# Down projection by Strassen's scheme, with split factors made once and kept in DRAM

## The chip, the cores and the metric

The program runs on one core of one Trainium2 chip. The metric is device time in microseconds (us) for one launch; lower is better. Engines are named as in the profile: PE (TensorE), PEld (its weight loads), DVE (VectorE), ACT (ScalarE), POOL (GpSimd), SP (SyncE, which issues most DMAs).

## What is computed

One decoder layer over 2048 prompt tokens and 32 sample tokens (2080 columns in all), in float32. What matters here is the channel mixer:

```
hn = rmsnorm(h)                         # 1024 features
u  = hn @ w_gate                        # 1024 -> 2816
c  = conv_b + 3-tap causal conv of u over tokens
h  = h + (silu(c) * (hn @ w_up)) @ w_down   # 2816 -> 1024
```

Ahead of it stand the input projections (a @ w_in, seven groups of 512 features), a gated linear recurrence, dilated attention and the output projection; behind it a gated embedding and a final norm.

## The kernel before, in words

Features lie on partitions, tokens on the free axis. A float32 operand is split into hi (rounded to the type that PE reads in one pass) and lo (the rest), and a product is three matmuls, hi\*hi, hi\*lo, lo\*hi: `mm3`, lines 136 to 138. So nearly every matmul of the program has one of these lines, and the tiles tell them apart.

- **Phase 0** (`in_phase(0, ...)`, first 1024 tokens): seven weight groups one after the other; a group's 8 weight tiles of 128x512 are loaded by SP (line 220), rounded on POOL (line 142) and subtracted on DVE (line 224). There are 4 buffers for raw tiles and 9 for rounded ones, so the last tiles of a group are loaded while PE changes over to it. Results leave by stores on SP (lines 265, 330, 337 to 342). Phase 1 does the same for the other 1056 tokens, with the recurrence (`hgrn_unit`) beside it; then come attention and sample work.
- **Trunk** (`trunk`): tokens in three blocks (`TRUNK`: 704, 704, 672). First the output projection for all blocks, then the channel mixer for all blocks (`ffn_block`), then the embedding (`embed_block`). A dense weight tile 128x512 comes by SP into a `raw` buffer, ACT copies its hi (line 909), DVE subtracts its lo (line 910).
- **Channel mixer of a block**: 22 feature tiles of 128, taken as 11 pairs. For a pair, gate and up are each one Strassen product of 2x2 quarters (`quarters`, `strassen`): seven products of 4 x 3 matmuls over half of the block's tokens, the sums of weight quarters on POOL (lines 1103 to 1111), the sums of results on DVE and ACT. The token factors of the block's input are made by `ffn_prep` at the change of block, ahead of the first pair. After conv, silu and gating (`gms`), the pair's activations are split (lines 1256 to 1259).
- **Down projection** (`downs`): for each pair, 8 output tiles x 2 token halves x 2 feature tiles x 3 matmuls = 96 matmuls, each result in a PSUM bank of its own, which DVE adds to `h` (line 1171). The weights of the pair are loaded and split anew in every block (4 tiles of 128x512). The 16 steps go into a queue `todo`; `down(n)` emits the next n of them between the products of the following pair's gate and up, as the tuples `gate` and `up` in `ffn_block` say. Steps left at a block's end are emitted in the next block's first pair.

The order on each engine is set by a list scheduler from program order, priorities and its own costs, so neighbouring work mixes more finely than the code.

Of the kernel before, what the change touches and what calls it, by code (L numbers as in the profile page):

```python
# [11 lines left out]
F32 = mybir.dt.float32  # L12
# [25 lines left out]
TRUNK = ((0, 704, 704), (704, 704, 704), (1408, 672, 640))  # L38
LAST = 256
LEVELS = (1, 4, 16)  # L40
USE = (1, 5, 6, 7, 4, 2, 3)
AHEAD = 1000
# [3 lines left out]
def hymba_step_kernel(ctx: ExitStack, tc: tile.TileContext, I: dict, O: dict):  # L46
# [37 lines left out]
    mix_d = dram.tile([128, NK, NTOK], F32, name="mix_d")  # L84
    h_d, hn_d, h2_d = [dram.tile([128, NK, NTOK], F32, name=n) for n in ("h_d", "hn_d", "h2_d")]
# [62 lines left out]
    def copy_after(ins, n=1):  # L148

        with tc.issue_after(ins.ins):  # L150
            for _ in range(min(n, len(copies))):
                src, dst, b, r = copies.pop(0)
                lo, hi = 292 * r, 292 * (r + 1)
                A.dma_start(O[dst][b, lo:hi], I[src][b, lo + 4:hi + 4])

# [21 lines left out]
    def in_phase(bi, tiles, shared, wp, ev, sm, pmm, pms, plv, po):  # L177
# [63 lines left out]
        def feature_group(g, kind, dst, w):  # L241
            todo = [(m, c0, cn) for c0, cn in chunks for m in range(4)]
            while todo:
# [10 lines left out]
                for (m, c0, cn), ps in zip(cur, pss):  # L254
# [10 lines left out]
                    SP.dma_start(dst[:, m, t0 + c0:t0 + c0 + cn], o)  # L265
# [14 lines left out]
        def token_group(g, kind, w):  # L280
            late = None

            for j in (0, 1, 8, 2, 3, 4, 5, 6, 7) if bi else range(8):
# [33 lines left out]
                if kind in "qk":  # L317
                    rotate(o, 16 if smp else tok // 128, n)

                    def late(o=o, n=n, smp=smp, tok=tok):  # L320
# [6 lines left out]
                        else:  # L327
                            oT = ev.tile([128, 4, 128], F32, name="oT", bufs=2)
                            V.tensor_copy(oT, ptv)
                            SP.dma_start((qT_d if kind == "q" else kT_d)[:, :, tok:tok + 128], oT)  # L330
# [4 lines left out]
                else:  # L335
                    if kind == "k":
                        SP.dma_start(O["pk"][tok:tok + 128], o)
                    if kind == "v":
                        SP.dma_start(O["pv"][tok:tok + 128], o)
                        SP.dma_start(v_d[tok:tok + 128], o)  # L340
# [557 lines left out]
    def trunk(cst, rp, ev, sm, tw, hp, sh, wp, pmm):  # L898
# [8 lines left out]
        def split(raw):  # L907
            w = wp.tile([128, 2, 512], F32R, name="w")
            A.copy(w[:, 0], raw)  # L909
            V.tensor_sub(w[:, 1], raw, f32(w[:, 0]))  # L910
            return w

        def weight(src):
            return [split(load(src[:, 512 * i:512 * i + 512])) for i in range(2)]
# [4 lines left out]

        def acc_tile():  # L920
            return pmm.tile([128, 512], F32, name="mm")

        def wide(T, dt=F32):
            return tw.tile([128, 704], dt, name="w")[:, :T]

        def held(T, dt=F32):
            return hp.tile([128, 704], dt, name="h")[:, :T]
# [170 lines left out]
        def quarters(src, f):  # L1098

            a11, a12, a21, a22 = [load(src[f + i][:, 512 * j:512 * j + 512]) for i in range(2) for j in range(2)]  # L1100
            w = {1: split(a11)}
            s1, s2 = raw_tile(), raw_tile()
            G.tensor_add(s1, a21, a22)  # L1103
            w[5] = split(s1)
            G.tensor_sub(s2, s1, a11)
            w[6] = split(s2)
            G.tensor_sub(a21, a11, a21)
            w[7] = split(a21)
            w[4] = split(a22)
            w[2] = split(a12)  # L1110
            G.tensor_sub(s2, a12, s2)  # L1111
            w[3] = split(s2)
            return w

        def strassen(w, X, H, put, after, before=lambda n: None):
# [8 lines left out]
            def copied():  # L1124
                t = sh.tile([128, 352], F32, name="s")[:, :H]
# [3 lines left out]
            pa, pb, pc = acc_tile(), acc_tile(), acc_tile()  # L1129
# [23 lines left out]
        def downs(b, f, parts, h):  # L1153
# [3 lines left out]
            w = [[], []]  # L1157

            def more():
                for i in range(2):  # L1160
                    j = len(w[i])
                    w[i].append(split(load(I["w_down"][f + i][:, 512 * j:512 * j + 512])))

            def one(m, c0):
                if (m, c0) == (2, 0):
                    more()
                cs = slice(c0, c0 + H)
                ps = acc_tile()
                for i, (hi, lo) in enumerate(parts):
                    mm3(ps[:, :H], *piece(w[i], m), hi[:, cs], lo[:, cs], i == 0, i == 1)  # L1170
                V.tensor_add(h[m][:, cs], h[m][:, cs], ps[:, :H])  # L1171
                if f == NF - 2 and c0:
                    SP.dma_start(h2_d[:, m, t0:t0 + T], h[m])

            more()
# [469 lines left out]
```

## Time and profile before

| | us |
|---|---|
| runs shown: median (lowest to highest) | 3101.7 (3099.03 to 3104.79) |
| the profiled execution's own time | 3096.28 |
| its span, first to last instruction | 3094.5 |
| PE busy | 2992.3 |
| DVE busy | 2233.4 |
| ACT busy | 1295.2 |
| POOL busy | 806.6 |

A matmul's record is longer than its turn on PE, since matmuls are pipelined: what one costs is read from how many fit into a stretch. Idle time of an engine matters only where PE waits for it.

### The profile page before, as it was taken

Reading aid. Unit: us, or ns where it says so; the run is one execution under the profiler, and the core shown is the slowest. Engines: PE = TensorE matmul, PEld = TensorE weight load, DVE = VectorE, ACT = ScalarE, POOL = GpSimd, SP = SyncE. Lnnn points to the kernel's source line nnn. Section 1 sums busy time; section 2 is a strip of 40 time slices with the busy share of each in tenths; the row PEclk is TensorE's granted clock in tenths of the full one; section 3 lists DMA queues with packets and bytes.
Section 4 is the critical chain, followed back from the end, with each engine's and each line's share of the span. In section 5 each row is a group of like instructions: output and inputs, shape, how many; then the busy total and the mean of one; then the engine's idle time right before and its main releaser. Section 6 shows DMA issues by size and latency. Waiting matters only on the chain.

```text
span 3094.5 us, 52057 instructions
## 1 busy us (share of the span) xinstructions
PE 2992.3 (97%) x19035; PEld 2785.2 (90%) x19035; DVE 2233.4 (72%) x4662; ACT 1295.2 (42%) x2813; POOL 806.6 (26%) x659
## 2 busy tenths in 40 slices
PE   9999999999889989999999999999999999999997
PEld 8988899987675667998999998999998999999997
DVE  7424667867587686568777779777789877777776
ACT  4111422222276564335444444444445444445443
POOL 1111122222343342002222232222222222222331
PEclk9999999999999999999999999999999999999998
DMA  5234333342539976673443445333434444436443
GB/s 185 93 121 135 105 104 104 106 141 81 158 79 284 285 225 218 237 265 139 137 133 113 133 156 168 124 126 131 144 119 162 153 139 139 144 116 219 132 166 130
DMA packets 265216, 467.97 MB, mean 151 GB/s; under 512 B 39360, under 2 KB 107072, under 8 KB 263168
## 3 DMA queue, kind: packets, MB, share of 16 engines
q1 hardware_dynamic: 261376, 397.66, 40.7%
q10 hardware_dynamic: 3584, 66.98, 6.1%
q8 instruction: 150, 2.46, 0.3%
q14 instruction: 106, 0.87, 0.1%
HBM read 381.05 MB, written 150.48 MB: 172 GB/s over the span
## 4 chain that ended last, share of the span: by engine, by line
PE 80%; DVE 12%; DMA 3%; issue 2%; ACT 1%; POOL 1%; SPq 0%; DVEq 0%; ACTq 0%; POOLq 0%
PE mm L136 18%; PE mm L137 18%; PE mm L138 18%; PE mm L301 3%; PE mm L302 3%; PE mm L303 3%; PE acc L744 1%; PE lv L441 1%; PE PT L732 1%; DVE w L910 1%; DVE P L724 1%; PE lv L301 1%; PE lv L303 1%; PE lv L302 1%; PE S L719 1%
## 5 line engine op out<-in xcount | busy, mean ns | idle before, releaser
L137 PE MATMUL mm<-w 128*128 128x352 f32 (+3 forms) x3768 | 1212.4, 322 | 4.3 <-DVE w L982 4.3
L138 PE MATMUL mm<-w 128*128 128x352 f32 (+3 forms) x3640 | 1164.0, 322 | 0.0
L136 PE MATMUL mm<-w 128*128 128x352 f32 (+3 forms) x3640 | 1138.7, 323 | 18.2 <-ACT w L981 8.7
L137 PEld LDWEIGHTS mm<-w 128*128 128x128 f32 x3768 | 712.9, 189 | 8.0 <-DVE w L982 7.8
L136 PEld LDWEIGHTS mm<-w 128*128 128x128 f32 x3640 | 681.8, 189 | 24.6 <-ACT w L981 10.6
L910 DVE TENSOR_TENSOR w<-raw,w 128x512 fp32r<-128x512 f32 x718 | 563.1, 799 | 179.5 <-ACT w L909 172.7
L138 PEld LDWEIGHTS mm<-w 128*128 128x128 f32 x3640 | 687.7, 189 | 0.1
L909 ACT CAST w<-raw 128x512 fp32r<-128x512 f32 x718 | 431.9, 620 | 396.3 <-PE mm L138 277.2
L1171 DVE TENSOR_TENSOR h<-h,mm 128x352 f32<-128x352 f32 (+1 forms) x528 | 257.6, 506 | 83.8 <-PE mm L138 83.2
L1103 POOL TENSOR_TENSOR raw<-raw 128x512 f32<-128x512 f32 x66 | 97.2, 1473 | 725.2 <-DMA raw<-in_w_gate_dram 251.0
L1111 POOL TENSOR_TENSOR raw<-raw 128x512 f32<-128x512 f32 x66 | 93.4, 1414 | 384.8 <-DVE w L910 384.8
L725 ACT ACTIVATE P<-P,st 128x256 f32<-128x256 f32 (+3 forms) x256 | 134.3, 527 | 75.5 <-DVE st L724 68.4
L1126 ACT COPY s<-mm 128x352 f32<-128x352 f32 (+1 forms) x198 | 88.2, 445 | 173.7 <-PE mm L138 169.2
L301 PE MATMUL mm<-wh,xh 128*128 128x512 f32 x352 | 142.0, 405 | 0.0
L303 PE MATMUL mm<-wh,xl 128*128 128x512 f32 x352 | 140.9, 401 | 0.0
L302 PE MATMUL mm<-wl,xh 128*128 128x512 f32 x352 | 140.4, 400 | 0.0
L142 POOL TENSOR_SCALAR wh<-wraw 128x512 fp32r<-128x512 f32 x96 | 72.0, 762 | 245.5 <-PE o L137 82.5
L136 PE MATMUL mm<-xh,wh 128*128 128x384 f32 (+2 forms) x384 | 124.9, 330 | 5.6 <-ACT xh L199 4.9
L724 DVE CUSTOM_DVE_ANT_0 P<-S,mask 128x256 f32<-128x256 f32 (+3 forms) x256 | 105.6, 445 | 29.7 <-PE S L720 25.3
L963 POOL TENSOR_TENSOR w<-w 128x704 f32<-128x704 f32 (+2 forms) x42 | 75.1, 1794 | 198.9 <-ACT w L962 198.2
L224 DVE TENSOR_TENSOR wl<-wraw,wh 128x512 fp32r<-128x512 f32 x104 | 84.6, 835 | 58.2 <-POOL wh L142 52.1
L138 PE MATMUL mm<-xh,wl 128*128 128x384 f32 (+2 forms) x384 | 125.1, 329 | 1.3 <-DVE wl L224 1.2
(337 smaller groups left out, 5156.3 us busy)
## 6 DMA issues: line engine op xcount, KB each, us to landing
raw<-in_w_gate_dram SPq DMA_DIRECT2D x132, 256.0 KB
raw<-in_w_up_dram SPq DMA_DIRECT2D x132, 256.0 KB
raw<-in_w_down_dram SPq DMA_DIRECT2D x132, 256.0 KB
out_sk_dram<-in_cache_k_dram ACTq DMA_DIRECT2D x56, 584.0 KB
out_sv_dram<-in_cache_v_dram ACTq DMA_DIRECT2D x56, 584.0 KB
wraw<-in_w_in_dram SPq DMA_DIRECT2D x104, 256.0 KB
raw<-in_w_ple_gate_dram SPq DMA_DIRECT2D x64, 256.0 KB
raw<-in_w_o_dram SPq DMA_DIRECT2D x48, 256.0 KB
```

The lines of the kernel that those rows point to most:

```text
L136: PE.matmul(ps, lhsT=wh, rhs=xh, start=first, stop=False, skip_group_check=read)
L137: PE.matmul(ps, lhsT=wh, rhs=xl, start=False, stop=False, skip_group_check=read)
L138: PE.matmul(ps, lhsT=wl, rhs=xh, start=False, stop=last, skip_group_check=read)
L301: PE.matmul(ps, lhsT=xh[k][:, js], rhs=wh, start=k == 0, stop=False)
L302: PE.matmul(ps, lhsT=xh[k][:, js], rhs=wl, start=False, stop=False)
L303: PE.matmul(ps, lhsT=xl[k][:, js], rhs=wh, start=False, stop=k == NK - 1)
L724: V.tensor_tensor_reduce(pe, s[:, w * i:w * i + w], bl.mask, 1.0, 3e38, ALU.add, ALU.min, mn)
L725: A.activation(pe, pe, AF.Exp, bias=mn, scale=-1.0, accum_out=st[:, bl.r, hh, 0:1])
L909: A.copy(w[:, 0], raw)
L910: V.tensor_sub(w[:, 1], raw, f32(w[:, 0]))
L1103: G.tensor_add(s1, a21, a22)
L1171: V.tensor_add(h[m][:, cs], h[m][:, cs], ps[:, :H])
```

## The change

The down projection of a pair becomes a Strassen product too. The pair's two feature tiles are the halves of the depth; output features (tiles 0 to 3 and 4 to 7) and token halves are the other two dimensions. So seven products of 4 output tiles x 3 matmuls take the place of the 96: 84 per pair. Two pairs are taken together (`group`), and their products add up in the same PSUM banks; the eleventh pair is alone.

- **Weights.** `down_weights` makes the seven split factors of every pair once, while phase 0 runs: 4 loads of 256 KB, 4 sums on POOL, 7 copies on ACT and 7 subtractions on DVE, and 7 stores of 512 KB to `wd_d` in DRAM, two factors per step of phase 0 from its ninth on. Loads and stores are on SP's queue. In the channel mixer `fetch` loads the factors with DMAs that POOL issues, into 5 buffers (`dw`).
- **Activations.** Four differences of half columns on POOL and seven split halves on ACT and DVE per pair take the place of two plain splits.
- **Results.** A bank holds a running sum: after products 1, 6, 7, 4 in turn DVE adds the bank to `h`, and the next product accumulates on top; products 5, 3 use the bank again, product 2 once more. So a product's matmuls wait until DVE has read the bank. Of the 8 banks, 4 are set apart for the down projection (`pdn`).
- **Steps.** 14 half products (two output tiles each) per group, 7 emitted per pair; at a block's end 21 are left instead of 16.
- **Buffers.** Blocks of 696, 696, 688 tokens; 7 raw and 6 split weight tiles instead of 8 and 9; 44 wide tiles instead of 40. The buffers of the recurrence are opened when `down_weights` is done.

```diff
-TRUNK = ((0, 704, 704), (704, 704, 704), (1408, 672, 640))
+TRUNK = ((0, 696, 696), (696, 696, 696), (1392, 688, 656))
+DOWN_USE = (1, 6, 7, 4, 5, 3, 2)
+    wd_d = [dram.tile([7, 128, 2, 512], F32R, name=f"wd{p}_d") for p in range(PAIRS)]
...
+    def down_weights(pool):
+        tile_ = lambda: pool.tile([128, 512], F32, name="draw", bufs=8)
+        for p in range(PAIRS):
+            a = [tile_() for _ in range(4)]
+            with tc.issue_after(recent[0].ins):
+                for x, (i, j) in zip(a, itertools.product(range(2), repeat=2)):
+                    SP.dma_start(x, I["w_down"][2 * p + j][:, 512 * i:512 * i + 512])
+            for n, w in factors(*a, tile_, lambda raw: split_to(pool.tile([128, 2, 512], F32R, name="dw", bufs=3), raw)):
+                SP.dma_start(f32(wd_d[p][n - 1]), f32(w))
+                yield
...
-        def downs(b, f, parts, h):
+        ADD = {1: (0, 0), 6: (0, 1), 7: (1, 1), 4: (1, 0), 5: (1, 1), 3: (0, 1), 2: (0, 0)}
+        def downs(b, ps, parts, h):
...
+            def fetch(i):
+                for n in DOWN_USE[i:i + 1]:
+                    w[n] = [dw.tile([128, 2, 512], F32R, name="w") for _ in ps]
+                    for t, p in zip(w[n], ps):
+                        G.dma_start(t, wd_d[p][n - 1])
+            def one(x, ms):
+                n = DOWN_USE[x]
+                if ms[0] == 0:
+                    fetch(x + 2)
+                i, j = ADD[n]
+                for m in ms:
+                    if n in (1, 5, 2):
+                        acc[m] = pdn.tile([128, 512], F32, name="mm")
+                    mk = slice(128 * m, 128 * m + 128)
+                    for y, (wt, X) in enumerate(zip(w[n], parts)):
+                        mm3(acc[m][:, :H], wt[:, 0, mk], wt[:, 1, mk], *X[n], n in (1, 5, 2) and y == 0,
+                            n in (4, 3, 2) and y == len(ps) - 1, n != 2)
+                for m in ms:
+                    o = h[m + 4 * i][:, H * j:H * j + H]
+                    V.tensor_add(o, o, acc[m][:, :H])
...
-            down(8)
+            down(7)
...
-                    gate, up = (0, 0, 1, 1, 1, 1, 1), (1, 2, 2, 2, 2, 1, 1)
+                    gate, up = (0, 1, 0, 1, 0, 1, 0), (1, 0, 1, 0, 1, 0, 1)
...
+    for i, _ in enumerate(in_phase(0, *args, plv, po)):
+        if i > 8:
+            step(down, 2)
+    step(down, 1000)
+    down_st.close()
...
-            ("tr", 8), ("tp", 9), ("ts", 1), ("th", 6), ("te", 2), ("tw", 40), ("thh", 8))]
+            ("tr", 7), ("tp", 6), ("dw", 5), ("ts", 1), ("th", 6), ("te", 2), ("tw", 44), ("thh", 8))]
```

Below, three places where the order of instructions moves. Lines of the changed program are other numbers: `mm3` is 140 to 142, the input weights' load 258, the store of a feature group 303, the weight sums 164 to 172.

**PE, second half of the channel mixer of a block.** Before, one bank of the down projection takes six matmuls and is done (behind the arrow the token tile stands first, then the weight tile; the numbers tell tiles apart):

```order
L136 MATMUL mm_20419<-w_20307,w_20331 128x352
...
L137 MATMUL mm_20419<-w_20308,w_20331 128x352
L138 MATMUL mm_20419<-w_20307,w_20331 128x352
L136 MATMUL mm_20419<-w_20300,w_20336 128x352
L137 MATMUL mm_20419<-w_20301,w_20336 128x352
L138 MATMUL mm_20419<-w_20300,w_20336 128x352
```

Now a bank is filled, read by DVE and filled further; these are products 1 and 6 of one group into one bank, with other work in the rows left out:

```order
L140 MATMUL mm_18806<-w_18280,w_18726 128x348
L141 MATMUL mm_18806<-w_18280,w_18726 128x348
L142 MATMUL mm_18806<-w_18280,w_18726 128x348
L140 MATMUL mm_18806<-w_18703,w_18727 128x348
L141 MATMUL mm_18806<-w_18703,w_18727 128x348
L142 MATMUL mm_18806<-w_18703,w_18727 128x348
...
L140 MATMUL mm_18806<-w_18285,w_18730 128x348
L141 MATMUL mm_18806<-w_18286,w_18730 128x348
L142 MATMUL mm_18806<-w_18285,w_18730 128x348
```

Between the sixth row and the seventh PE has 42 other matmuls, and DVE has the addition that frees the bank.

**SP, phase 0, at the change from the second group to the third** (`ha_d<-ev` a result's store, `wraw` an input weight's load, `draw` a down weight's load, `wd_d<-dw` a factor's store). Before:

```order
L220 DMA wraw_1286<-in_w_in_dram 128x512
L265 DMA ha1_d_82<-ev_1219 128x384
L220 DMA wraw_1292<-in_w_in_dram 128x512
L220 DMA wraw_1298<-in_w_in_dram 128x512
...
L265 DMA ha1_d_82<-ev_1250 128x384
L220 DMA wraw_1688<-in_w_in_dram 128x512
```

Now:

```order
L303 DMA ha1_d_82<-ev_1234 128x384
L189 DMA draw_1240<-in_w_down_dram 128x512
L189 DMA draw_1241<-in_w_down_dram 128x512
L191 DMA wd1_d_86<-dw_1161 128x1024
L189 DMA draw_1242<-in_w_down_dram 128x512
L189 DMA draw_1243<-in_w_down_dram 128x512
L191 DMA wd1_d_86<-dw_1165 128x1024
L303 DMA ha1_d_82<-ev_1284 128x384
L191 DMA wd1_d_86<-dw_1200 128x1024
L258 DMA wraw_1417<-in_w_in_dram 128x512
L303 DMA ha1_d_82<-ev_1325 128x384
L258 DMA wraw_1423<-in_w_in_dram 128x512
```

The loads of the input weights now stand behind factor stores that wait for DVE, and the queue holds such stores until near the end of the sixth group.

**POOL, channel mixer.** Before, it has the weight sums alone:

```order
L1103 TENSOR_TENSOR raw_17128<-raw_17121,raw_17123 128x512
L1107 TENSOR_TENSOR raw_17121<-raw_17117,raw_17121 128x512
L1105 TENSOR_TENSOR raw_17129<-raw_17128,raw_17117 128x512
L1111 TENSOR_TENSOR raw_17129<-raw_17119,raw_17129 128x512
```

Now it has the differences of activations (`u<-w`) and the factor loads between them:

```order
L164 TENSOR_TENSOR raw_17650<-raw_17643,raw_17645 128x512
L1315 TENSOR_TENSOR u_17416<-w_17201 128x348
L1318 TENSOR_TENSOR u_17417<-w_17207,w_17201 128x348
L168 TENSOR_TENSOR raw_17643<-raw_17639,raw_17643 128x512
L166 TENSOR_TENSOR raw_17651<-raw_17650,raw_17639 128x512
L1316 TENSOR_TENSOR u_17416<-w_17207,u_17416 128x348
L1193 DMA w_17396<-wd3_d_88 128x1024
L1193 DMA w_17549<-wd2_d_87 128x1024
L1319 TENSOR_TENSOR u_17417<-w_17207,u_17416 128x348
L1193 DMA w_17550<-wd3_d_88 128x1024
L1193 DMA w_17864<-wd4_d_89 128x1024
L172 TENSOR_TENSOR raw_17651<-raw_17641,raw_17651 128x512
```

Each of the four loads waits until PE has given a `dw` buffer back, and the last weight sum stands behind them.

## Rows read from the trace of the kernel before

**Rows 1.** The page: busy us (share of the span) and instructions of each engine, and PE's busy tenths in 40 slices of the span.

```profile
PE 2992.3 (97%) x19035; PEld 2785.2 (90%) x19035; DVE 2233.4 (72%) x4662; ACT 1295.2 (42%) x2813; POOL 806.6 (26%) x659
PE   9999999999889989999999999999999999999997
```

**Rows 2.** Stretches of the channel mixer: start:end and length in us, then busy us (and instructions) of PE, PEld, DVE, ACT, POOL, then PE's granted clock, the DMA engines' share and GB/s. Blocks of 704, of 672, and the whole mixer.

```profile
1900.00:2300.00 400.00, 400.00 (x2500) 400.00 (x2500) 301.54 (x454) 179.35 (x346) 113.92 (x77) 1.00 0.40 133
2380.00:2780.00 400.00, 400.00 (x2609) 400.00 (x2608) 317.10 (x533) 192.45 (x419) 117.33 (x80) 1.00 0.41 137
1406.00:2830.00 1424.00, 1402.97 (x8785) 1393.61 (x8784) 1127.51 (x1763) 664.85 (x1316) 403.36 (x264) 0.99 0.42 140
```

**Rows 3.** Groups of instructions in 1900 to 2300 us, shapes apart: line, engine, operation, tiles, shapes, count, then busy us, mean ns of one, and idle time before them with what ended it.

```profile
L910 DVE TENSOR_TENSOR w<-raw,w 128x512 fp32r<-128x512 f32 x171 | 133.0, 792 | 40.8 <-ACT w L909 38.8
L1171 DVE TENSOR_TENSOR h<-h,mm 128x352 f32<-128x352 f32 x146 | 72.6, 513 | 33.6 <-PE mm L138 33.5
L1246 DVE SCALAR_TENSOR_TENSOR w<-u,taps,w 128x704 f32<-128x704 f32 x20 | 26.1, 1303 | 0.0
L1259 DVE TENSOR_TENSOR w<-w 128x704 fp32r<-128x704 f32 x18 | 15.9, 886 | 0.0
L1107 POOL TENSOR_TENSOR raw<-raw 128x512 f32<-128x512 f32 x19 | 33.5, 1763 | 0.8
L1111 POOL TENSOR_TENSOR raw<-raw 128x512 f32<-128x512 f32 x20 | 29.2, 1462 | 112.2 <-DVE w L910 112.2
L1103 POOL TENSOR_TENSOR raw<-raw 128x512 f32<-128x512 f32 x19 | 27.9, 1466 | 180.5 <-DMA raw<-in_w_down_dram 77.1 <-DMA raw<-in_w_gate_dram 47.8 <-DVE w L910 24.2
L1105 POOL TENSOR_TENSOR raw<-raw 128x512 f32<-128x512 f32 x19 | 26.3, 1384 | 10.7 <-DVE w L910 10.0
```

**Rows 4.** Phase 0 from the end of its start to the end of its sixth group, columns as in rows 2.

```profile
45.00:275.00 230.00, 230.00 (x1233) 206.96 (x1232) 93.67 (x207) 34.57 (x65) 35.47 (x46) 1.00 0.36 116
```

**Rows 5.** Who waited for whom from 0 to 330 us (engine, line, releaser: us in total, times, longest): all of PE's rows, and the rounding of input weights.

```profile
PE mm L136 <- ACT xh L199: 4.9, 1, 4.9
PE lv L136 <- ACT xh L199: 2.0, 2, 1.8
PE mm L137 <- DVE xl L200: 0.8, 2, 0.4
...
POOL wh L142 <- DMA wraw<-in_w_in_dram: 15.6, 13, 2.6
```

**Rows 6.** The page's DMA issues: the down weights.

```profile
raw<-in_w_down_dram SPq DMA_DIRECT2D x132, 256.0 KB
```

**Rows 7.** The DMA view of two stretches in which the engines are full: 2936 to 2952 us (whole rows of 2.6 KB, loads and stores), then 1016 to 1032 us (with short rows and copies to many partitions).

```profile
DMA packets 2317, 5.45 MB, mean 340 GB/s; under 512 B 255, under 2 KB 255, under 8 KB 2316
q1 hardware_dynamic: 2316, 5.43, 92.8%
...
DMA packets 2553, 4.07 MB, mean 254 GB/s; under 512 B 189, under 2 KB 783, under 8 KB 2552
```

**Rows 8.** Issues of one load on SP's queue: count, ns min/median/max.

```profile
L220 SPq DMA_DIRECT2D wraw<-in_w_in_dram x104: 327/332/1340, 1.2 to 762.5; - x104
```

**Rows 9.** The changes of block in the channel mixer and its end, columns as in rows 2; then two groups of DVE in 1850 to 1900 us, as in rows 3.

```profile
1850.00:1900.00 50.00, 43.81 (x243) 41.19 (x242) 49.36 (x81) 24.36 (x43) 13.21 (x8) 0.90 0.56 188
2327.00:2380.00 53.00, 47.10 (x263) 44.64 (x262) 52.13 (x86) 26.20 (x51) 15.35 (x8) 0.90 0.51 170
2780.00:2830.00 50.00, 48.41 (x311) 47.34 (x310) 44.59 (x70) 28.01 (x48) 14.22 (x7) 1.00 0.60 201
...
L1171 DVE TENSOR_TENSOR h<-h,mm 128x352 f32<-128x352 f32 x24 | 11.5, 508 | 0.0
L910 DVE TENSOR_TENSOR w<-raw,w 128x512 fp32r<-128x512 f32 x15 | 10.8, 736 | 0.1
```

**Rows 10.** The chain that ended last, where attention ends and the trunk begins: start us, us, what.

```profile
1211.41 2.95 DMA coef_d<-wt
1214.38 0.45 SPq L676
1214.88 3.83 DMA cf<-coef_d
1218.87 2.53 POOL o L681 x2
1221.43 0.79 ACT w L981
```

**Rows 11.** The last stretch of the embedding, columns as in rows 2, and the three things that PE waited for from 2930 us on.

```profile
3000.00:3094.50 94.50, 74.22 (x470) 72.77 (x468) 65.44 (x158) 31.92 (x64) 14.36 (x16) 0.86 0.42 142
PE mm L123 <- DVE rs_y L99: 6.0, 2, 3.5
PE mm L123 <- DVE rs_v L114: 4.6, 2, 4.1
PE mm L108 <- DVE w L963: 2.2, 1, 2.2
```

More of the change, by code (lines that the diff above doesn't have):

```diff
@@ L905, in load, with split, weight @@
             return raw
[L907 to L914, printed above, removed]
+        def split(raw, pool=wp):
+            return split_to(pool.tile([128, 2, 512], F32R, name="w"), raw)
+        def weight(src, pool=wp):
+            return [split(load(src[:, 512 * i:512 * i + 512]), pool) for i in range(2)]
         def piece(w, j):
@@ L1098, in quarters @@
         def quarters(src, f):
[L1100 to L1113, printed above, removed]
+            a = [load(src[f + i][:, 512 * j:512 * j + 512]) for i in range(2) for j in range(2)]
+            return dict(factors(*a, raw_tile, split))
         def strassen(w, X, H, put, after, before=lambda n: None):
@@ L1124, in copied @@
             def copied():
[L1125 removed]
+                t = sh.tile([128, 348], F32, name="s")[:, :H]
                 A.copy(t, pa[:, :H])
                 return t
[L1129 removed]
+            pa, pb, pc = [pmm.tile([128, 512], F32, name="mm") for _ in range(3)]
             product(pa, 1)
@@ L1317, in embed_block @@
             more()
-            wpp = [weight(I["w_ple_proj"][128 * k:128 * k + 128]) for k in range(2)]
+            wpp = [weight(I["w_ple_proj"][128 * k:128 * k + 128], dw) for k in range(2)]
             ssq = wide(T)
@@ L1416, in hymba_step_kernel @@
     plv, po = pool("h_plv", 3, space=PSUM), pool("h_po", 1, space=PSUM)
-    pool = pools(hgrn_st, side="right")
-    hc, ld, wk, sp = pool("h_c", 1), pool("h_l", 2), pool("h_w", 2), pool("h_s", 2)
-    S = []
-    for h in range(4):
-        s = sp.tile([128, 128], F32, name=f"S{h}")
-        G.memset(s, 0.0)
-        S.append(s)
+    down_st = ExitStack()
+    down = down_weights(pools(down_st, side="right")("dn", 1))
     def from_pool(pool, *names):
@@ L1446, in begin @@
         return hgrn(0, 4, *psum)
-    for _ in in_phase(0, *args, plv, po):
-        pass
+    for i, _ in enumerate(in_phase(0, *args, plv, po)):
[3 more added lines that the diff above has]
+    down_st.close()
+    pool = pools(hgrn_st, side="right")
+    hc, ld, wk, sp = pool("h_c", 1), pool("h_l", 2), pool("h_w", 2), pool("h_s", 2)
+    S = []
+    for h in range(4):
+        s = sp.tile([128, 128], F32, name=f"S{h}")
+        G.memset(s, 0.0)
+        S.append(s)
+    msk = hc.tile([128, 9, 128], U8, name="msk")
     side = begin()
```

115 lines of the change are left out of this document (72 added, 43 removed).

## The prediction

> **What bounds the kernel now.** I read the page first: PE is busy for 97% of the span, and its slices show nines nearly throughout, the others are well below [rows 1]. Then the stretches of the channel mixer, where the change acts: inside a block PE is busy for 400 of 400 us, 2500 matmuls of 352 columns, so 0.160 us each, and 2609 of 336 columns, 0.1533 us each [rows 2]. There a matmul taken out is time taken out, as long as DVE (75%), POOL (28%) and the DMA engines (40%) keep up. Then phase 0, where the new work is put: PE is busy for all of 230 us there, DVE for 41%, ACT 15%, POOL 15%, the DMA engines 36% [rows 4], and PE's only waits are those of the kernel's start [rows 5]. Last the places where PE is not the limit: the changes of block, where DVE is busy for 49.4 of 50 us and 52.1 of 53 [rows 9], the step from attention to trunk, a chain through DMAs and POOL [rows 10], and the end, where PE works 74 of 94 us [rows 11].
>
> **The sum.** It is made against the profiled execution, 3096.3 us (span 3094.5); the median of the runs shown is 5.4 us above that, and the forecast is put back by as much.
>
> *Matmuls.* Per block 11 pairs x 96 become 11 x 84; with the 168 of gate and up a block has 2772 matmuls instead of 2904. Between the two prices of rows 2 a column costs 0.42 ns, so 348 columns take 0.1583 us and 344 take 0.1567. Before: 2904 x (0.160 + 0.160 + 0.1533) = 1374.5 us; after: 2772 x (0.1583 + 0.1583 + 0.1567) = 1312.1. **-62.4 us.** The columns of all other trunk stages add up to the same 2080: 0.
>
> *DVE and ACT inside a block.* Per pair, DVE loses 4 weight splits (4 x 0.79) and 2 of 16 additions (2 x 0.51), and gains one and a half splits of activations (1.5 x 0.89) [rows 3]: -2.8 us of a pair's 32. The four half-width products instead of two full ones are the same elements. ACT moves the same way. No cost, beside PE.
>
> *POOL inside a block.* Two Strassen products need 2 x (1.76 + 1.46 + 1.47 + 1.38) = 12.2 us of sums per pair [rows 3]; the four new differences are 348 columns wide, by the mean of those rows 1.52 x 348/512 = 1.03 us each, 4.1 in all. Of a pair's 252 x 0.158 = 39.9 us that leaves 23.6 us for 7 factor loads, 3.4 us each. No DMA is issued by POOL in this trace. The nearest row is an issue on SP: 0.33 us, at the longest 1.34 [rows 8]. Within that nothing is late: 0. The other end is a rival below.
>
> *DMAs inside a block.* The down weights go: 132 x 256 KB = 34.6 MB [rows 6]. 231 factor loads of 512 KB come: 121.1 MB. Full engines moved 340 GB/s at a share of 0.93, so 366 GB/s with whole rows [rows 7]; the net 86.5 MB are 236 us of engine time. The mixer's share was 0.42 of 1424 us [rows 2], 598 us; it becomes 834 of some 1360, or 0.61. A factor is asked for two products ahead, four half products of which 7 share 40 us, so some 23 us: 0.
>
> *Phase 0.* Onto DVE come 77 x 0.79 = 61 us, onto POOL 44 sums, 67 us at 1.52: 155 and 102 of 230, no bound. DMAs: 77 stores of 512 KB and 44 loads of 256 KB are 51.9 MB, 142 us at 366 GB/s, beside 0.36 x 230 = 83 us that are there [rows 4]. Together 225 of 230 us: the engines are full from the second group to the sixth. The order of instructions puts the input weights of five groups behind such stores in SP's queue. Their rounding waited for its load 13 times, 15.6 us in all, and PE lost nothing by it [rows 5], since it goes on with other tiles. With full engines each load lands later. Bounds: 0 if PE always finds a tile; and at the 254 GB/s of the other full stretch [rows 7] the 51.9 MB need 204 us, 287 in all, 57 too many. The transfers here are whole rows of 2 and 4 KB, like the first stretch, so the volume just fits, and I take two microseconds at each of five changes of group: **+10 us** (0 to 57).
>
> *Changes of block.* Steps left over are 7 half products of 12 matmuls and 14 of 6 instead of 16 of 6, 72 matmuls more, 11.4 us of PE; DVE gets 42 additions instead of 16, 26 x 0.508 = 13.2 us, less a pair's four splits, 4 x 0.736 = 2.9 [rows 9], and plus the last pair's half split more of activations. DVE is the limit there, PE has room: +11.6 against +11.4, nothing lost by volume. But the lone pair's products follow each other with 12 matmuls (1.9 us) each, and each needs the 4 additions (2.0 us) of the one before: I take 1 us at each of two changes and the end, **+3** (0 to 3 x 13.2 = 40).
>
> *Attention to trunk.* Five factor loads (2.6 MB, 7.2 us of full engines) stand on POOL ahead of the last sums of attention, whose chain runs through two DMAs and POOL [rows 10]. If a copy of 3.83 us has to share the engines with them it can double: **+2** (0 to 7). The constants of the sample attention move from there to the start of the program, which takes load off: inside these bounds.
>
> *The end.* Six split tiles instead of nine: at three weights per group start all six are taken. PE idles 20 of 94 us there for other reasons [rows 11]. **+2** (0 to 10).
>
> Sum: -62.4 + 10 + 3 + 2 + 2 = -45.4. 3096.3 - 45.4 = 3050.9, and with the 5.4 us to the median **3056 us**. With the terms' smaller ends the likeliest case reaches down to 3040, and I let it go up to 3072.
>
> **Rivals.**
> 1. *PE waits for the banks.* A product may not start until DVE has emptied the bank of the one before. In the order there are 42 matmuls, 6.6 us, between two products on a bank, DVE needs 0.51 us for the addition but is busy three quarters of the time and has operations of 1.3 us [rows 3]. 126 products give 252 half steps; at 0.1 us each that is 25 us. For it: nothing had to be emptied in time before, with eight banks for all. Against: 6.6 us is long. Time: 3072 to 3092, say 3080.
> 2. *Phase 0 is bound by its DMAs.* The 57 us above in place of the 10: 3103, no change. For it: 98% full by the better rate, in-order queue. Against: rows of 4 KB.
> 3. *POOL becomes the bound, and the kernel slower.* From 3.4 us per factor load on, each pair lasts as long as POOL needs: every 0.1 us more costs 33 x 7 x 0.1 = 23 us. The forecast's gain of 45 us is gone at 3.6 us; at 4 us per load the time is 3056 + 139 = 3195. For it: its issue price stands in no row, and POOL works in order, so that a load waiting for its buffer holds up the weight sums behind it. Against: SP's longest issue is 1.34 us. The Trainium skill, "SBUF — State Buffer", section "SBUF: two separate sides", says that descriptors of a DMA from GpSimd's queue are written by GpSimd's own cores, which are shut out while DVE holds the port they share, and its section on bandwidth pools gives some 620 ns for a DMA alone and 3100 ns beside a DVE copy. By that figure POOL would need 7 x 3.1 + 16.3 = 38.0 us of a pair's 39.9, an estimate: just no bound, and the sum would stay. No row here can bear it out.
> 4. *More is gained.* If phase 0 hides everything and shorter DVE queues shorten the changes of block too: below 3040. That the matmuls don't go away is no case: the order of instructions has 396 fewer in the mixer.
>
> **How the numbers follow.** The likeliest case (3040 to 3072) gets 0.66: its term is large and rests on rows, the others are small beside it. Rival 1 gets 0.14, rival 2 gets 0.06, rival 3 gets 0.08, rival 4 gets 0.06. About 0.2% (6 us) is what a measurement can tell from no change. Faster: 0.66 + 0.14 + 0.06 = 0.86; same: 0.06; slower: 0.08. A range of 3040 to 3092 holds the first two, 0.80.
>
> **What the profile after would show.** Right: in the middle of a block PE is busy throughout at 0.158 us per matmul and a pair of gate, up and down takes 40 us; `raw<-in_w_down` falls to 44 issues; phase 0 ends within 15 us of where it did, with the DMA share above 0.9; POOL's queue shows issues under 2 us. Wrong: PE waiting for line 1209's additions in mid-block (rival 1); PE idle at the changes of group in phase 0 with SP's queue waiting for DVE (rival 2); POOL's idle time gone and PE waiting for split weights (rival 3). I am wrong most cheaply in the sizes of phase 0 and of the changes of block.

## The result, and the profile after

The changed kernel takes 3084.7 us, the median of five runs (3080.4 to 3090.4), against 3101.5 for the kernel before: a ratio of 0.9948 with a 95% interval of 0.9931 to 0.9964. That is 16.8 us less where the sum had 45.4. The profiled execution is the longest of its five, 3090.4 us with a span of 3088.6.

The page of the kernel after: busy us and instructions of each engine, and PE's busy tenths, to set beside [rows 1].

```profile
PE 2952.6 (96%) x18639; PEld 2736.8 (89%) x18639; DVE 2322.6 (75%) x4715; ACT 1304.4 (42%) x2824; POOL 1150.1 (37%) x1066
PE   8999999999889899999999998999999999999998
```

396 matmuls are gone, as forecast, but PE's busy time fell by 39.7 us, not by 62.4, and a slice inside the mixer (the 25th) is at 8, where none was. The stretches of the kernel after, columns as in rows 2: phase 0, two pieces of a block of 696 and of the one of 688, and the whole mixer.

```profile
45.00:275.00 230.00, 225.62 (x1206) 202.51 (x1205) 152.82 (x253) 71.49 (x130) 93.09 (x81) 1.00 0.85 306
2120.00:2300.00 180.00, 180.00 (x1132) 180.00 (x1132) 145.19 (x211) 77.21 (x148) 90.45 (x85) 1.00 0.61 200
2420.00:2780.00 360.00, 358.92 (x2273) 358.29 (x2272) 300.91 (x480) 171.97 (x373) 173.97 (x166) 1.00 0.61 201
1406.00:2830.00 1424.00, 1371.84 (x8483) 1359.36 (x8482) 1158.38 (x1768) 637.76 (x1261) 682.33 (x626) 0.99 0.61 200
```

Beside [rows 4], phase 0 now keeps the DMA engines at 0.85 and DVE at 66%, and PE loses 4.4 us. Beside [rows 2], there are stretches in the mixer where PE is full, as forecast, and the whole mixer is not: PE idles 52 of 1424 us where it idled 21. What PE waited for there (1432 to 2829 us: engine, line, releaser: us in total, times, longest):

```profile
PE mm L140 <- DMA w<-wd_d: 15.9, 6, 5.8
PE mm L140 <- ACT s L1151: 11.5, 5, 3.4
PE mm L140 <- DVE w L1122: 4.6, 1, 4.6
PE mm L140 <- DVE w L1124: 4.6, 1, 4.6
PE mm L140 <- DVE u L1166: 3.0, 1, 3.0
PE mm L140 <- DVE h L1209: 2.6, 7, 0.7
```

The largest group is one that the forecast had at nothing, the waits for factor loads (`w<-wd_d`): five in mid-block (0.5 to 5.8 us) and one at the mixer's end. The other large ones stand within 90 us behind the start of a block. The additions that empty the banks (line 1209, rival 1) are 2.6 us in seven pieces. The loads themselves: count, ns min/median/max of an issue, then what POOL's idle time before them waited for.

```profile
L1193 POOL DMA_DIRECT2D w<-wd_d x231: 527/544/746, 1214.0 to 2812.0; - x116
...
  PE mm L142: 192.1, 71
...
DMA to landing us min/median/max: 3.7/6.0/14.6
```

An issue costs POOL 0.54 us, far under the 3.4 us from which rival 3 would have decided. But a load can take 14.6 us to land, and POOL stands 192 us before such issues until PE frees a buffer. Two of PE's stops, in steps of 4 us, columns as in rows 2:

```profile
1700.00:1704.00 4.00, 4.00 (x27) 4.00 (x27) 1.76 (x4) 1.75 (x3) 3.98 (x5) 1.00 0.61 166
1704.00:1708.00 4.00, 4.00 (x27) 4.00 (x26) 4.00 (x8) 3.22 (x7) 1.10 (x2) 1.00 0.96 374
1708.00:1712.00 4.00, 1.55 (x10) 1.26 (x8) 2.46 (x4) 1.16 (x3) 1.30 (x1) 0.99 1.02 392
1712.00:1716.00 4.00, 3.43 (x12) 3.43 (x13) 0.52 (x1) 0.00 (x0) 0.00 (x0) 0.50 1.06 337
2008.00:2012.00 4.00, 4.00 (x27) 4.00 (x27) 2.42 (x4) 1.62 (x3) 3.99 (x6) 1.00 0.27 78
2012.00:2016.00 4.00, 4.00 (x27) 4.00 (x26) 2.84 (x5) 2.40 (x5) 2.77 (x2) 1.00 1.02 317
2016.00:2020.00 4.00, 1.39 (x9) 1.09 (x7) 3.85 (x6) 1.89 (x6) 1.67 (x3) 1.00 0.95 351
2020.00:2024.00 4.00, 0.77 (x3) 0.77 (x4) 0.00 (x0) 0.00 (x0) 0.00 (x0) 0.82 1.01 342
```

At both the DMA engines (second column from the right) are full for some 12 us. After the first stop, in which PE stood for 3 us, TensorE is granted 1.2 GHz (0.50 from 1712 to 1716): 12 matmuls take 3.43 us, 0.29 each where 0.159 is the price at 2.4 GHz. What fills the engines at the second stop: the queues of 2010 to 2024 us (packets, MB, share of the 16 engines; q10 has the cache copies, q0 the factor loads, q1 the loads of gate and up) and the DMA issues (count, KB each, median us to landing), then POOL's work in order of time (start us, us).

```profile
q10 hardware_dynamic: 127, 2.39, 45.2%
q0 software_dynamic: 335, 1.26, 31.3%
...
out_sk_dram<-in_cache_k_dram ACTq DMA_DIRECT2D x4, 584.0 KB
w<-wd_d POOLq DMA_DIRECT2D x4, 512.0 KB, 12.1
raw<-in_w_gate_dram SPq DMA_DIRECT2D x2, 256.0 KB
```

```profile
1991.52 1.11 POOL L1193 DMA_DIRECT2D w<-wd_d  x2
...
2009.54 1.40 POOL L1316 TENSOR_TENSOR u<-w,u 128x348 f32<-128x348 f32 x1
2010.87 1.11 POOL L1193 DMA_DIRECT2D w<-wd_d  x2
2011.98 1.54 POOL L1319 TENSOR_TENSOR u<-w,u 128x348 f32<-128x348 f32 x1
2014.76 1.87 POOL L172 TENSOR_TENSOR raw<-raw 128x512 f32<-128x512 f32 x1 [1.23 <-DVE w L177]
2016.56 1.11 POOL L1193 DMA_DIRECT2D w<-wd_d  x2
```

A product of two pairs needs two factor tiles, and POOL issues their loads in the program's order, so that the 231 issues of the trace can be counted off. At each of the five stops in mid-block PE stood for the same one: the second tile of a group's sixth product (product 3). At the second stop shown, PE stood from 2017.4 us on. The first tile of that product had been issued at 1992.1, as the second of the two issues in the first row: 25 us ahead, much as forecast. The second tile was issued at 2010.9, 6.5 us ahead; at the other four stops it was 7.7 to 8.2 us. Loads two products ahead of PE need six tiles, and there are five buffers: the sixth tile has to wait until PE gives one back, and it stands behind the step's differences and weight sums in POOL's order; the trace doesn't tell which of the two held it longer. Right beside it ScalarE issued four copies of the cache (`copy_after`, at the splits of the same differences). So two things meet, a late issue and full engines, and the experiments take away one or the other.

### The profile page after: what moved, and what is told of

Its sections match the earlier page's. It is cut to its first block, busy times and chain, and to the rows that moved or that the text cites. A ratio compares the mean times of both kernels' runs of the same rounds, so it can differ in the third digit from the quotient of the medians.

```text
span 3088.6 us, 51939 instructions
## 1 busy us (share of the span) xinstructions
PE 2952.6 (96%) x18639; PEld 2736.8 (89%) x18639; DVE 2322.6 (75%) x4715; ACT 1304.4 (42%) x2824; POOL 1150.1 (37%) x1066
## 3 DMA queue, kind: packets, MB, share of 16 engines
q0 software_dynamic: 33264, 121.13, 12.3%
q10 hardware_dynamic: 3584, 66.98, 5.9%
## 4 chain that ended last, share of the span: by engine, by line
PE 43%; DVE 8%; issue 3%; DMA 3%; POOL 2%; ACT 1%; DVEq 0%; ACTq 0%; POOLq 0%; SPq 0%
PE mm L140 14%; PE mm L142 14%; PE mm L141 14%; DMA w<-wd_d 2%; DVE w L177 2%; DVE h L1209 1%; DVE w L1285 1%; DVE w L1286 1%; POOL raw L164 1%; DVE w L1352 1%; POOL raw L168 0%; ACT w L176 0%; DMA raw<-in_w_up_dram 0%; POOL raw L166 0%; DVE w L1019 0%
## 5 line engine op out<-in xcount | busy, mean ns | idle before, releaser
L141 PE MATMUL mm<-w 128*128 128x348 f32 (+3 forms) x3636 | 1173.7, 323 | 2.2 <-DVE w L1352 1.7
L140 PE MATMUL mm<-w 128*128 128x348 f32 (+3 forms) x3508 | 1114.7, 325 | 52.2 <-DMA w<-wd_d 15.9
L142 PE MATMUL mm<-w 128*128 128x348 f32 (+3 forms) x3508 | 1124.3, 323 | 2.3 <-DVE w L177 2.3
L140 PEld LDWEIGHTS mm<-w 128*128 128x128 f32 x3508 | 662.3, 190 | 63.5 <-DMA w<-wd_d 15.8
L141 PEld LDWEIGHTS mm<-w 128*128 128x128 f32 x3636 | 690.5, 190 | 5.8 <-DVE w L1352 2.6
L142 PEld LDWEIGHTS mm<-w 128*128 128x128 f32 x3508 | 664.4, 190 | 3.7 <-DVE w L177 3.0
L177 DVE TENSOR_TENSOR w<-raw,w 128x512 fp32r<-128x512 f32 x586 | 524.1, 904 | 164.9 <-ACT w L176 159.1
L176 ACT CAST w<-raw 128x512 fp32r<-128x512 f32 x586 | 359.1, 620 | 373.9 <-PE mm L142 267.7
L1209 DVE TENSOR_TENSOR h<-h,mm 128x348 f32<-128x348 f32 (+1 forms) x504 | 243.8, 505 | 47.7 <-PE mm L142 47.0
L164 POOL TENSOR_TENSOR raw<-raw 128x512 f32<-128x512 f32 x66 | 101.3, 1535 | 471.3 <-DMA w<-hn_d 153.0
L1193 POOL DMA_DIRECT2D w<-wd_d x231 | 127.5, 554 | 217.8 <-PE mm L142 192.1
L172 POOL TENSOR_TENSOR raw<-raw 128x512 f32<-128x512 f32 x66 | 96.8, 1467 | 195.2 <-DVE w L177 185.5
L1000 POOL TENSOR_TENSOR w<-w 128x696 f32<-128x696 f32 (+2 forms) x42 | 74.8, 1789 | 169.2 <-ACT w L999 168.4
L141 PE MATMUL mm<-xl,wh 128*128 128x384 f32 (+2 forms) x384 | 124.5, 327 | 1.7 <-DVE xl L238 1.7
L1151 ACT COPY s<-mm 128x348 f32<-128x348 f32 (+1 forms) x198 | 87.6, 442 | 79.6 <-PE mm L142 75.6
```

The source lines that it names most:

```text
L140: PE.matmul(ps, lhsT=wh, rhs=xh, start=first, stop=False, skip_group_check=read)
L141: PE.matmul(ps, lhsT=wh, rhs=xl, start=False, stop=False, skip_group_check=read)
L142: PE.matmul(ps, lhsT=wl, rhs=xh, start=False, stop=last, skip_group_check=read)
L1193: G.dma_start(t, wd_d[p][n - 1])
L1209: V.tensor_add(o, o, acc[m][:, :H])
```

## The experiments

Times are against the kernel before, measured on the same chip each time (medians 3098.4, 3100.7 and 3100.3 us); gains in us are the ratio's, taken of 3101.5. "Mixer" is the time between equal matmuls of the sequence (the 8771st from the start, the 1511th from the end) in the one profiled execution.

| kernel | median us | ratio (95% interval) | gain us | mixer us |
|---|---|---|---|---|
| before | 3101.5 | 1 | 0 | 1415.1 |
| the change | 3084.7 | 0.9948 (0.9931 to 0.9964) | 16 | 1401.7 |
| e1, no factor loads | 3059.6 | 0.9874 (0.9859 to 0.9888) | 39 | 1376.8 |
| e2, lone pair first | 3081.9 | 0.9946 (0.9933 to 0.9958) | 17 | 1392.0 |
| e3, six buffers | 3070.8 | 0.9913 (0.9897 to 0.9928) | 27 | 1382.5 |
| e4, no making | 3076.8 | 0.9929 (0.9915 to 0.9942) | 22 | 1397.8 |
| f1, lone first, six | 3063.9 | 0.9881 (0.9865 to 0.9897) | 37 | 1371.5 |
| f2, lone first, seven | 3067.7 | 0.9893 (0.9874 to 0.9912) | 33 | 1374.3 |
| f3, quarter loads | 3093.4 | 0.9979 (0.9966 to 0.9992) | 7 | 1406.3 |
| f4, none, lone first | 3050.2 | 0.9837 (0.9822 to 0.9852) | 51 | 1355.5 |
| g1, copies spread | 3064.5 | 0.9886 (0.9870 to 0.9902) | 35 | 1378.8 |
| g2, lone, six, spread | 3056.8 | 0.9861 (0.9843 to 0.9880) | 43 | 1365.9 |
| g3, f4 with nine tiles | 3044.1 | 0.9818 (0.9800 to 0.9835) | 56 | 1351.1 |
| g4, before with spread | 3099.2 | 1.0000 (0.9989 to 1.0011) | 0 | 1419.1 |

**e1, no factor loads.** `fetch` loads two tiles once and hands them out for every product:

```diff
-                    w[n] = [dw.tile([128, 2, 512], F32R, name="w") for _ in ps]
-                    for t, p in zip(w[n], ps):
-                        G.dma_start(t, wd_d[p][n - 1])
+                    if not kept:
+                        ...
+                    w[n] = kept[:len(ps)]
```

> The changed kernel with its factor loads in the mixer left out: two factor tiles are loaded once and used for every product (so the down products are not those of the reference); matmuls, additions, gate and up are as they were. Theory A (the lost time is in the loads: POOL's in-order queue stands 192 us before them until a buffer is free, they land after TensorE has come to the product, 16.3 us of stops, and the clock is at 1.2 GHz for 6.8 us behind three of them): all stops on the factors go, and POOL's sums for gate and up come earlier too; 3055 to 3068 us. Theory B (the change of block: 42 additions on VectorE where there were 16): only the 16 us of named stops go, 3066 to 3075. Theory C (six split tiles for gate and up instead of nine leave TensorE no lead, so that every burst of VectorE reaches it): 3072 to 3085.

Measured: a gain of 39 us instead of 16. So 23 us (16 to 30) are the loads' (theory A), more than the 15.9 us of named waits. Of the rest some 6 us can be the clock, an estimate: behind two of the change's stops in mid-block TensorE was granted 1.2 GHz for 6.8 us each (from 1712.0 and from 2022.6 us), and without the loads it never was in mid-block. What PE waits for then in the mixer (columns as above; its two largest rows):

```profile
PE mm L140 <- ACT s L1151: 16.0, 10, 3.9
PE mm L141 <- DVE w L1355: 2.6, 1, 2.6
```

**e2, the lone pair first.** `if len(group) == 2 or last:` becomes `if len(group) == 2 or f == 0:`.

> The changed kernel with the pairs grouped as tile pair 0 alone, then (1,2) to (9,10), so that the lone one is done in mid-block, and at a change of block 14 half products of 12 matmuls are left over, with 28 additions instead of 42. Theory B (change of block bound by VectorE's additions): 14 x 0.51 = 7 us less of VectorE at each of three changes, and the stops there (4.7 + 3.4 + 2.7 us after 1870, 4.8 + 1.5 + 3.2 us after 2340) mostly go: 3062 to 3074. Theory A (late factor loads): the stops in mid-block stay, 3078 to 3088. Theory C: some gain, 3074 to 3082.

Measured: no change in time. The stops at the changes of block became smaller, but two stops on factors of 6 us each came in mid-block. They again stood for the second tile of the sixth product. A gain at one place was paid back at another, so this run alone decides nothing on theory B.

**e3, six factor buffers.** `("dw", 5)` becomes 6, `("tw", 44)` becomes 43.

> The changed kernel with six buffers for factors instead of five (and 43 instead of 44 of the wide ones): a factor asked for two products ahead then takes a buffer of the product before, which is done, so POOL's queue need not wait. Theory A: POOL's idle time before its loads falls from 218 us to under 30, the stops on factors from 16 us to under 5, with the clock behind them 3062 to 3074. Theory B and C: POOL's wait goes, but the time stays within 3079 to 3089.

Measured: 27 us, 11 more than the change (4 to 18) and inside theory A's range, with 5.6 us of stops on factors, all at changes of block. But one of its rows failed: POOL still waits long before the loads (first row below).

```profile
  PE mm L142: 165.1, 67
...
1990.39 1.11 POOL L1193 DMA_DIRECT2D w<-wd_d  x2
```

POOL runs ahead of PE there. Its wait is not itself the loss; a load that is issued or lands too late is. The second row shows what the sixth buffer changes: both tiles of the sixth product are issued together now, where the change's second tile came 19 us behind the first. The cache copies are where they were and loads still take up to 14.6 us to land, but no stop on factors is left in mid-block. So the late issue is needed for these stops.

**e4, factors of one pair only.** `for p in range(PAIRS)` in `down_weights` becomes `range(1)`, and every load reads `wd_d[0]`.

> The changed kernel with factors made for one pair only, in phase 0, and every load in the mixer reading that pair's (so the down products are not those of the reference); ten of eleven makings with their loads and stores are left out. By the places of equal matmuls phase 0 costs 5.2 us at matmul 700 and 6.5 us at its end: expected 3077 to 3080, with the first matmul after phase 0 back at 322 us. The prediction's term was 10 us: 3073 to 3076. If the drift of another 5 us before the attention also comes from it: 3071 to 3074.

Measured: 6 us more gain than the change (by the two intervals, -1 to 12). TensorE's first weight loads in HGRN stand for the end of phase 0: count, ns min/median/max, first and last start us, of the kernel before, the change and e4.

```profile
L441 PEld LDWEIGHTS lv<-hM,hF x336: 186/189/192, 321.5 to 735.0; 128*128 128x128 f32 x168
```

```profile
L479 PEld LDWEIGHTS lv<-hM,hF x336: 186/189/192, 328.6 to 743.7; 128*128 128x128 f32 x168
```

```profile
L479 PEld LDWEIGHTS lv<-hM,hF x336: 186/189/192, 322.5 to 737.4; 128*128 128x128 f32 x168
```

The eleven kernels that make all factors stand there at 326.1 to 328.6 us, e4 at 322.5. Making the factors costs some 4 to 6 us, in phase 0.

**f1 and f2, both edits, six and seven buffers** (42 and 41 wide ones).

> Tile pair 0 alone first and six factor buffers together (42 wide ones). Against the kernel before on the same chip the change itself stood at -16 us, six buffers alone at -28, lone first alone at -16. With six buffers the stops left on factors were three of 2 us, all where the last pair's products follow each other at a change of block; lone first takes those away. If that is so, and VectorE has 14 additions less at each change: -32 to -37. If lone first only moves stops to other places, as it did with five buffers: -25 to -30.

> As the one with six buffers and lone first, with seven factor buffers and 41 wide ones. If what is left of the loss is POOL's queue standing before the loads (165 us with six buffers), its idle time there falls under 60 us and the time is 4 to 8 us below the six-buffer kernel's. If what is left is VectorE and ScalarE at the start of a block, the time is the same within 3 us; should 41 wide buffers be too few, TensorE waits at the change of block and it is over 4 us longer.

Measured: f1 gains 37 us, 10 more than e3 (3 to 17). With no stop on factors left, lone first does count. The two largest waits of PE in f1's mixer:

```profile
PE mm L140 <- ACT w L1306: 8.6, 5, 4.5
PE mm L142 <- DVE w L177: 7.6, 7, 3.3
```

A seventh buffer (f2) brings nothing that can be told from noise, and POOL's wait, 126 us in f1, stays at 117 us.

**f3, quarter loads.** The loads and the products take columns 0 to 127 only:

```diff
-                        G.dma_start(t, wd_d[p][n - 1])
+                        G.dma_start(t, wd_d[p][n - 1][:, :, 0:128])
```

> The changed kernel with each factor load cut to the first 128 of 512 columns, a quarter of the bytes in 512-byte pieces; the products use these columns four times over (so the down products are not those of the reference). Issues, buffers and POOL's waits for them are as they were. Theory A1 (the loads' bytes: 121 MB beside gate's and up's loads make a load land 10 to 14 us after its issue at times): landing mostly under 5 us, stops on factors under 4 us, and the time is near the kernel without loads: -35 to -40 us against the kernel before. Theory A2 (POOL's order: a load is issued too late, and sums for gate and up stand behind its wait): POOL's idle time before the loads stays near 190 us, and the time stays at -16 to -24.

Measured: neither. It is 9 us slower than the change (3 to 16). Its loads:

```profile
L1193 POOL DMA_DIRECT2D w<-wd_d x231: 713/722/922, 1215.8 to 2817.5; - x116
...
DMA to landing us min/median/max: 2.5/3.6/12.4
```

The median landing fell, the longest hardly did (14.6 to 12.4 us). A load of 128 KB still takes up to 12.4 us, so at those places it is not its own bytes that it waits for. And PE waits more often, 22.8 us in ten stops, though the loads bring a quarter of the bytes. The edit changed a second thing, though: cut into pieces of 512 bytes, the loads have 62832 packets instead of 33264, so this run doesn't part bytes from packets, and why it is slower than the change stays open. What else was in flight gave theory A3: ahead of each of f3's five stops of over 1 us in mid-block, and of the change's four, the four cache copies of a step (584 KB each) had been issued within 10 us; ahead of f3's stop of over 1 us at a change of block none had.

**f4, no loads and lone first.** Both edits together, with four factor buffers and 41 wide ones.

> Without factor loads (two tiles loaded once, so the down products are not those of the reference) and tile pair 0 alone first, with 41 wide buffers. Without loads alone the kernel stood at -39 us against the kernel before. If the additions left over at a change of block cost what is still missing (stops of 3.1, 1.5, 1.5 us after 1909 and 1.1, 1.6, 1.6, 4.1 us after 2362, and 2.8 us at 2783): -44 to -50. If those stops come from the start of a block itself, with gate's and up's six split tiles: -36 to -41.

Measured: 51 us, 11 more than e1 (5 to 18). The lone pair's place at the end of a block costs some 10 us once the loads no longer hide it (f1 against e3: 10). PE over the two changes of block, of the change, of f1 and of f4, columns as in rows 2:

```profile
1840.00:1960.00 120.00, 108.86 (x640) 106.57 (x639) 102.31 (x160) 54.08 (x99) 50.04 (x48) 0.94 0.68 222
2320.00:2440.00 120.00, 109.67 (x666) 106.87 (x665) 105.03 (x178) 54.62 (x110) 53.25 (x50) 0.97 0.64 206
```

```profile
1830.00:1950.00 120.00, 112.30 (x685) 110.01 (x685) 104.55 (x163) 52.31 (x97) 51.84 (x50) 0.99 0.67 228
2310.00:2430.00 120.00, 112.10 (x679) 109.64 (x678) 107.47 (x176) 54.99 (x117) 53.69 (x51) 0.97 0.67 221
```

```profile
1830.00:1950.00 120.00, 117.23 (x723) 114.57 (x722) 110.86 (x171) 56.97 (x107) 41.66 (x31) 1.00 0.43 144
2310.00:2430.00 120.00, 114.23 (x708) 111.52 (x708) 109.01 (x182) 59.14 (x124) 41.87 (x31) 1.00 0.43 138
```

In 120 us at the first change PE gets through 640, 685 and 723 matmuls, at the second through 666, 679 and 708.

**g1, the copies spread.** The copies move from the activations' splits to the strassen copies, one behind `s1` and one behind `s3`, of gate and of up:

```diff
-            s1 = copied()
+            s1, c = copied()
+            copy_after(c, n)
...
-                pair(5, 6, t, 2 if f < NF - 4 else 0)
+                pair(5, 6, t)
...
-                pair(7, 4, u, 2 if f < NF - 2 else 0)
+                pair(7, 4, u)
```

> The changed kernel, with the four cache copies of a step (584 KB each), which ScalarE issues two and two right beside the splits of the activations, spread over the step: one behind the first and the third copied product of gate and of up. Issues, bytes and buffers stay. Theory A3 (the factor loads asked for at a step's end share full engines with the four copies: 1704 to 1716 and 2012 to 2024 the DMA share is 1.0, and loads take 10 to 14 us to land): no load takes over 9 us, stops on factors under 4 us, -26 to -32 us against the kernel before (the change itself: -16). Theory A2 (only POOL's order counts: loads are issued too late because they stand behind buffers and differences): stops on factors at least 10 us, -13 to -20.

Measured: 35 us, 19 more than the change (12 to 26), with the same bytes, issues and buffers. The second tile of the sixth product is still issued some 17 us behind the first (1997.7 and 1980.8 in the second block's first group), but it lands in 3.9 us instead of 12.3. Two stretches of mid-block, 1500 to 1840 and 1980 to 2290 us, of the kernel before, of the change and of g1:

```profile
1500.00:1840.00 340.00, 339.88 (x2124) 339.60 (x2123) 257.23 (x388) 149.91 (x288) 93.50 (x65) 1.00 0.39 128
1980.00:2290.00 310.00, 310.00 (x1939) 310.00 (x1938) 230.07 (x348) 137.53 (x264) 84.14 (x59) 1.00 0.38 128
```

```profile
1500.00:1840.00 340.00, 334.08 (x2074) 332.95 (x2075) 265.13 (x385) 145.40 (x284) 172.00 (x158) 0.99 0.60 200
1980.00:2290.00 310.00, 301.18 (x1872) 300.60 (x1872) 239.48 (x344) 130.73 (x253) 151.57 (x139) 0.99 0.59 195
```

```profile
1500.00:1840.00 340.00, 340.00 (x2138) 340.00 (x2137) 273.57 (x395) 153.48 (x298) 174.28 (x162) 1.00 0.61 207
1980.00:2290.00 310.00, 310.00 (x1951) 310.00 (x1950) 245.81 (x360) 135.99 (x264) 156.80 (x149) 1.00 0.61 203
```

g1 has PE full for all 650 us and does 143 matmuls more in them than the change, 22.7 us at 0.159. The time from issue to landing fell (first row), and of PE's waits in the mixer the loads keep this much (second row):

```profile
DMA to landing us min/median/max: 3.7/4.7/10.6
```

```profile
PE mm L140 <- DMA w<-wd_d: 13.1, 4, 6.2
```

The stops on factors expected to be under 4 us are 13.1, but the large ones stand at the changes of block (6.2 us up to 1867, 3.9 up to 2325, 2.8 up to 2773), where the lone pair's products follow each other; none is in mid-block. The longest landing, 10.6 us where at most 9 was expected, is at the start of the trunk. Where the change's engines were full from 2012 to 2024, g1's share from 2003 to 2019 is 0.51. So the full engines are needed for the stops in mid-block, as the late issue is.

**g2, all three edits.** Lone first, six buffers, copies spread.

> Tile pair 0 alone first, six factor buffers and the copies spread. Without the spread this kernel had no stop on factors and stood at -37 us against the kernel before. If the copies' bursts also delay the weights of gate and up (stops of 3.3 and 1.7 us on weight splits), -41 to -47; if they hurt only through the factor loads, -34 to -40.

Measured: 3056.8 us, the fastest kernel here that does the whole computation, and faster than both given ones. Against f1 the spread's own part (6 us) is not clear from zero.

**g3, nine split tiles.** f4 with `("tp", 6)` at 9.

> As the kernel without factor loads and with tile pair 0 alone first (two tiles loaded once, so the down products are not those of the reference; it stood at -50 us against the kernel before), with nine split tiles for gate's and up's weights as before the change, in place of six. Theory C (six tiles leave too little lead): the stops that are left in the mixer (24 us) fall to under 14, -57 to -64. If six are enough: -47 to -53.

Measured: 56 us, 6 more than f4, where the intervals still overlap. So theory C's part is -1 to 13 us and stays open.

**g4, control.** The kernel before with its copies spread.

> Control: the kernel before, with its cache copies spread in the same way. Its down weights were asked for on the other queue and had nine tiles; its mixer stood still at the changes of block only. If the bursts matter only where a factor load is just in time: within 3 us of the kernel before. If spreading helps any kernel: 5 to 12 us less.

Measured: 1.0000 (0.9989 to 1.0011). Spreading the copies gains nothing in the kernel before, within some 3 us either way; the bursts cost where a load is just in time.

## Why the prediction was wrong

- **Matmuls, -62.4.** The count was right, the price not. I drew a line between the prices at 336 and at 352 columns [rows 2]; it gave 0.1583 us at 348 and 0.1567 at 344. Measured in full stretches: 650/4089 = 0.1590 (g1's rows; 0.1591 in e1, without loads) and 358.92/2273 = 0.1579. 5544 x 0.1590 + 2772 x 0.1579 = 1319 against 1374.5 before: **-55**, 7 us less gain.
- **DVE, ACT and POOL inside a block, 0.** Right: with the copies spread PE is full in mid-block, with DVE at 80% and POOL at 51%. Rival 3 falls with its price: 231 issues, none over 0.75 us. The Trainium skill's 3100 ns beside a DVE copy ("SBUF — State Buffer", section "A bandwidth-pool intuition that's wrong (but worth ruling out)") is told there of a whole DMA; I had put it in for an issue, and no issue here took as long.
- **DMAs inside a block, 0. This is the step that failed**: "a factor is asked for two products ahead [...] some 23 us: 0". I had set the mean share of the engines, 0.61, which came out at 0.61, against a lead counted in program order. The lead of 23 us held for the first of a product's two tiles (25). For the second it is 6.5 to 8.2 us where a step ends, since two products ahead need six tiles and there are five buffers, and POOL's queue works off the step's differences and weight sums first. There the engines are not at 0.61 but full, since `copy_after` puts four copies beside those differences, and the load takes 8 to 12 us to land. With either of the two taken away no stop on factors is left in mid-block (e3, g1). Taking the loads away gave 23 us, spreading the copies alone 19, the sixth buffer alone 11; why the last is less is not known.
- **Phase 0, +10.** Measured 6 (e4; 328.6 against 321.5 us in the rows). The sign I named, a DMA share above 0.9, was not met: 0.85. Nor is the wait the one I had reckoned with: PE waited 3.3 us in four pieces for DVE's part of the input weights (line 262), and for no load itself.
- **Changes of block, +3.** Too small: some 10 (f1 against e3, 3 to 17; f4 against e1, 5 to 18), inside the bounds of 0 to 40. That the lone pair at a block's end costs is shown. Part of it is factor loads that follow each other faster than they land (5.6 us in e3, none in f1). That the rest is DVE's additions is not shown: PE waited 1.8 us for them in e1 and 3.2 in f4, and what fell is its wait for ACT's copies of products, from 17.3 us to 7.6 (1420 to 2830 us), which is 4.1 in the kernel before (line 1126 there). Whether it matters there that gate and up now share four banks instead of eight, no run tests.
- **Attention to trunk +2, end +2.** Neither can be told from noise: the mixer's first matmul comes 10.5 us later than before, of which 8.7 are there at the end of HGRN (743.7 against 735.0 in e4's rows), and from the 1511th matmul before the end on the changed kernel takes 258.9 us and the kernel before 261.9.
- **Rivals.** The time lies outside the likeliest case (3040 to 3072) and in the whole range only by the part kept for rival 1. That was luck: rival 1 named the right size of time (3080) with the wrong wait, since the banks are 2.6 us. Rivals 2, 3 and 4 did not come about.

With the measured terms the sum is -55 + 6 + 19 + 10 = -20, an estimate beside the measured -16.

## What to carry to other kernels

A load's lead is the time between its issue on its own queue and its use in the trace, not the number of steps between them in the program: look at what stands ahead of it in that queue, and count the buffers that so many steps ahead need. A mean DMA share says little; look at the share in the few microseconds in which the tightest load flies, and at what else the program issues at the same event. Bulk copies that nobody waits for belong where no load is due. And an edit that brings nothing beside a larger stop (e2) can bring 10 us when that is gone (f1).

## What the runs showed of the hardware

- A load of 128 KB took up to 12.4 us beside four copies of 584 KB. The page of the change has 3584 packets and 66.98 MB for the copies' queue at 5.9% of 16 engines' span: 18.7 KB and 0.81 us a packet, two per engine and copy, so four copies hold each engine 6.5 us (an estimate from these rows). The Trainium skill, "DMA: Bandwidth & Descriptors", section "Queues, rings and completion order", says that an engine takes turns between queues packet by packet. By that a load would pay for the turns of its packets more than for its bytes. f3's longest landing, with a quarter of the bytes and nearly twice the packets, fits this; no run here shows the turns themselves.
- A quarter of a load, in 512-byte pieces (f3), cost POOL 0.72 us an issue instead of 0.54 for the whole in pieces of 4 KB.
- A matmul's price, read from full stretches, was not on a line in its columns: 0.1533 us at 336, 0.1579 at 344, 0.1590 at 348, 0.1600 at 352. Why was not tried.
- Between equal matmuls of the start and of the mixer's beginning, profiles of kernels with the same program there differ by up to 11 us (8.2 us behind the kernel before in e1's, 19.0 in e3's), with no difference in their medians to match. One profile is no measure of an effect of that size.
